# Longer weight runs, quarter-lane casts on two engines, and another order of loads in a batched matrix product

## Chip, cores, metric

One core of one Trainium2 chip (trn2). The metric is the device time of one execution in microseconds (us), median of several executions.

## The reference

```python
b1, b2, m, k, n = 8, 16, 256, 512, 384
x      : (8, 16, 256, 512) float32
weight : (8, 16, 512, 384) float32
return np.matmul(x, weight).astype(np.float32)
```

That is 128 independent products of 256x512 by 512x384. The kernel works on 32 groups of G = 4 products. A group loads 2.10 MB of x and 3.15 MB of weights and stores 1.57 MB.

## The kernel before

Five engines run their own programs and meet at semaphores (counters that one engine raises and another waits for). SyncE (SP) issues all transfers. ScalarE (ACT) casts x to bf16 and copies results out of PSUM, the memory that TensorE writes its results to. VectorE (DVE) casts weights and copies the transposed x out of PSUM. TensorE (PE) transposes and multiplies. GpSimd only makes the identity matrix for the transposes.

```python
def load(e, t, U, s):                       # SP: w, w, x
    n = t * U + s
    for d in range(G // D):                 # two loads of two products each
        slot = (s * (G // D) + d) % WS
        if not isinstance(n, int) or n >= 2:
            e.wait_ge(w_cast, n * (G * S) + ((d + 1) * D * S - 2 * G * S))
        e.dma_start(w_sb[slot][:],          # 128 partitions, 8 rows of w each: 12 KB runs
            w_rows[...].rearrange("(p k) n -> p k n", k=S * KO)).then_inc(w_in[slot], 16)
    ...                                     # then x, 16 KB runs
def prepare(e, t, U, s):                    # DVE
    ...
    for a in range(D):
        for h in range(S):                  # 8 casts per group, each 64 lanes x 1536
            e.tensor_copy(out=w_bf[...][h * HP : (h + 1) * HP],
                          in_=w_sb[slot][a * HP : (a + 1) * HP, h * KO : (h + 1) * KO, :],
                          ).then_inc(w_cast, 1)
    for q in range(T): ...                  # 4 copies x_t <- pt
def on_sync(e):
    ...
    for s in range(U):
        load(e, t, U, LAG + s)              # LAG = 4 groups ahead
        store(e, t, U, s)
def on_scalar(e):
    ...                                     # 4 casts x_bf <- x_sb, then 4 copies out_sb <- po
```

Of the kernel before, what the change touches and what calls it, by code (L numbers as in the profile page):

```python
# [12 lines left out]
def kernel(  # L13
# [6 lines left out]
    nc = tc.nc  # L20
    P = 128

    b1, b2, M, K = x.shape
    _, _, _, N = weight.shape
    B = b1 * b2
    KO = K // P

    x_rows = x.rearrange("b1 b2 m k -> (b1 b2 m) k")
    w_rows = weight.rearrange("b1 b2 k n -> (b1 b2 k) n")
    o_rows = out.rearrange("b1 b2 m n -> (b1 b2 m) n")  # L30

    fp32 = mybir.dt.float32
    bf16 = mybir.dt.bfloat16
# [3 lines left out]



    G = 4  # L40
    C = P // G
    R = G * M // P
    T = R // 2
    D = 2
    S = 2
    HP = P // D
    NG = B // G

    XS, WS, OS = 2, 2 * G // D, 4
    BS, TS, WBS = 1, 2, 2 * G  # L50
    PT, PO = 4, 2

    LAG = 4

    ctx.enter_context(tc.tile_critical(no_gpsimd_drain=True))  # L55

    def sbuf(name, shape, dtype, n):
        return [
            ctx.enter_context(nc.sbuf_tensor(f"{name}{s}", shape, dtype)) for s in range(n)
        ]  # L60
# [6 lines left out]
    def sems(name, n):  # L67
        return [tc.alloc_semaphore(f"{name}{s}") for s in range(n)]
# [2 lines left out]
    identity = sbuf("identity", [P, P], fp32, 1)[0]  # L71
    x_sb = sbuf("x_sb", [P, R, K], fp32, XS)

    x_bf = sbuf("x_bf", [P, R, S, HP, KO], bf16, BS)
    x_t = sbuf("x_t", [P, R, KO // 2, P, 2], bf16, TS)
    w_sb = sbuf("w_sb", [P, S * KO, N], fp32, WS)
    w_bf = sbuf("w_bf", [P, KO, N], bf16, WBS)
    out_sb = sbuf("out_sb", [P, R, N], fp32, OS)
    pt = psum("pt", [P, 2, KO // 2, P], fp32, PT)
# [2 lines left out]



    id_done, x_cast, w_cast, t_made, t_copied, p_made, o_copied = (
        sems(name, 1)[0]
        for name in (
            "id_done", "x_cast", "w_cast", "t_made", "t_copied", "p_made", "o_copied"
        )
    )  # L90
    x_in, w_in, o_out = sems("x_in", XS), sems("w_in", WS), sems("o_out", OS)


    BIAS = 8


    def load(e, t, U, s):
        n = t * U + s
        for d in range(G // D):
            slot = (s * (G // D) + d) % WS  # L100
            if not isinstance(n, int) or n >= 2:
                e.wait_ge(w_cast, n * (G * S) + ((d + 1) * D * S - 2 * G * S))
            e.dma_start(  # L103
                w_sb[slot][:],
                w_rows[bass.ds(n * (G * K) + d * (D * K), D * K)].rearrange(
                    "(p k) n -> p k n", k=S * KO
                ),
            ).then_inc(w_in[slot], 16)
        if not isinstance(n, int) or n >= XS:
            e.wait_ge(x_cast, n * T + (1 - XS) * T)  # L110
        e.dma_start(  # L111
            x_sb[s % XS][:],
            x_rows[bass.ds(n * (G * M), G * M)].rearrange("(p r) k -> p r k", r=R),
        ).then_inc(x_in[s % XS], 16)

    def store(e, t, U, s, pieces=1):
        n = t * U + s
        dram = o_rows[bass.ds(n * (G * M), G * M)].rearrange("(p r) n -> p r n", r=R)
        for q in range(pieces):
            rows = slice(q * R // pieces, (q + 1) * R // pieces)  # L120
            e.wait_ge(o_copied, n * T + ((q + 1) * T // pieces + BIAS))
            e.dma_start(out=dram[:, rows], in_=out_sb[s % OS][:, rows]).then_inc(
                o_out[s % OS], 16
            )

    def cast_x(e, t, U, s, q):
        n = t * U + s
        if q == 0:
            e.wait_ge(x_in[s % XS], (t * (U // XS) + s // XS) * 16 + 16)
        e.wait_ge(t_made, n * T + (q + 1 - T + BIAS))  # L130
        rows = slice(2 * q, 2 * q + 2)
        e.copy(  # L132
            out=x_bf[s % BS][:, rows],
            in_=x_sb[s % XS][:, rows].rearrange("p r (q s c) -> p r s q c", s=S, c=KO),
        ).then_inc(x_cast, 1)

    def prepare(e, t, U, s):
        n = t * U + s
        e.wait_ge(p_made, n * T + (BIAS - T))
        for d in range(G // D):  # L140
            slot = (s * (G // D) + d) % WS
            e.wait_ge(
                w_in[slot], (t * (U * G // D // WS) + s * G // D // WS) * 16 + 16
            )
            for a in range(D):
                for h in range(S):
                    e.tensor_copy(  # L147
                        out=w_bf[(s * G + d * D + a) % WBS][h * HP : (h + 1) * HP],
                        in_=w_sb[slot][a * HP : (a + 1) * HP, h * KO : (h + 1) * KO, :],
                    ).then_inc(w_cast, 1)  # L150
        for q in range(T):
            e.wait_ge(t_made, n * T + (q + 1 + BIAS))
            e.tensor_copy(  # L153
                out=x_t[s % TS][:, 2 * q : 2 * q + 2],
                in_=pt[(s * T + q) % PT][:].bitcast(bf16),
            ).then_inc(t_copied, 1)

    def multiply(e, t, U, s):
        n = t * U + s
        words = x_bf[s % BS][:].rearrange("p r s q c -> p r (s q c)").bitcast(fp32)  # L160
        for q in range(T):
            e.wait_ge(x_cast, n * T + (q + 1))
            e.wait_ge(t_copied, n * T + (q + 1 - PT + BIAS))
            for rr in range(2):
                for h in range(KO // 2):
                    ins = e.transpose(  # L166
                        pt[(s * T + q) % PT][:, rr, h, :],
                        words[:, 2 * q + rr, h :: KO // 2],
                        identity[:],
                    )  # L170
            ins.then_inc(t_made, 1)
        e.wait_ge(w_cast, n * (G * S) + G * S)
        for q in range(T):
            e.wait_ge(t_copied, n * T + (q + 1 + BIAS))
            e.wait_ge(o_copied, n * T + (q + 1 - PO + BIAS))
            for rr in range(2):
                for ko in range(KO):
                    for i in range(G):
                        mine = slice(i * C, (i + 1) * C)
                        ins = e.matmul(  # L180
                            po[(s * T + q) % PO][mine, rr, :N],
                            x_t[s % TS][:, 2 * q + rr, ko // 2, mine, ko % 2],
                            w_bf[(s * G + i) % WBS][:, ko, :],
                            start=(ko == 0),
                            stop=(ko == KO - 1),
                        )
            ins.then_inc(p_made, 1)

    def copy_out(e, t, U, s, q):
        n = t * U + s  # L190
        if q == 0:
            e.wait_ge(o_out[s % OS], (t * (U // OS) + s // OS) * 16 + 16)
        e.wait_ge(p_made, n * T + (q + 1 + BIAS))  # L193
        e.copy(  # L194
            out=out_sb[s % OS][:, 2 * q : 2 * q + 2, :],
            in_=po[(s * T + q) % PO][:, :, :N],
        ).then_inc(o_copied, 1)
# [7 lines left out]
    def on_sync(e):  # L205
        U = OS
        for n in range(LAG):
            load(e, 0, NG, n)
        rounds = (NG - LAG) // U
        with e.Fori(0, rounds) as t:  # L210
            for s in range(U):
                load(e, t, U, LAG + s)
                store(e, t, U, s)
        for n in range(rounds * U, NG):
            if n + LAG < NG:
                load(e, 0, NG, n + LAG)
            store(e, 0, NG, n, T if n == NG - 1 else 1)
        for s in range(OS):
            e.wait_ge(o_out[s], 16 + 16 * (NG // OS + (T - 1 if s == (NG - 1) % OS else 0)))

    def on_vector(e):
        U = 2
        e.sem_inc(t_copied, BIAS)
        with e.Fori(0, NG // U) as t:
            for s in range(U):
                prepare(e, t, U, s)

    def on_tensor(e):
        U = 2
        e.sem_inc(t_made, BIAS)  # L230
        e.sem_inc(p_made, BIAS)
        e.wait_ge(id_done, 2)

        pe = mybir.EngineType.PE
        with nc.Fori(0, NG // U, engines=OrderedEngineSet([pe]), head_slot={pe: 0}) as t:
            for s in range(U):
                multiply(e, t, U, s)

    def on_scalar(e):
        U = OS  # L240
        e.sem_inc(o_copied, BIAS)
        for s in range(OS):
            e.sem_inc(o_out[s], 16)

        with e.Fori(0, NG // U) as t:
            for s in range(U):
                for q in range(T):
                    cast_x(e, t, U, s, q)
                for q in range(T):
                    copy_out(e, t, U, s, q)  # L250

    on_gpsimd(nc.gpsimd)
    on_sync(nc.sync)
    on_vector(nc.vector)
    on_tensor(nc.tensor)
    on_scalar(nc.scalar)


# [28 lines left out]
```

## Time and profile before

| | before |
|---|---|
| time, median of 4 | 518.26 us (517.97 to 518.42) |
| span of the profiled run | 517.2 us (that run took 518.98 us) |
| DMA queue, share of 16 engines | 99.3% |
| DVE, ACT, PE busy | 64%, 46%, 59% |

The lines behind this table stand in the prediction below. The reader should take one thing from them: the 16 DMA engines are busy throughout, and every other engine waits on them.

### The profile page before, as it was taken

The numbers are of one execution on the slowest core, as the hardware profiler recorded it, in microseconds if no ns is written. First come the engines' busy times: TensorE is split into PE (matmuls) and PEld (weight loads), VectorE is DVE, ScalarE is ACT, GpSimd is POOL, SyncE is SP. The second block draws the span as 40 slices with busy tenths as digits, with TensorE's granted clock in tenths as the row PEclk, the third lists the DMA queues.
The fourth block names the chain that finished last, engine by engine and source line by source line (L and its number), as shares of the span: only waits on it lengthen the run. The fifth ranks groups of instructions, "written<-read, shape, count | busy, mean of one in ns | idle before, by whom it ended". The sixth has DMA issues, their size and how long they took to land.

```text
span 517.2 us, 11523 instructions
## 1 busy us (share of the span) xinstructions
PE 306.6 (59%) x4608; PEld 200.6 (39%) x4608; DVE 332.8 (64%) x384; ACT 236.7 (46%) x264; POOL 0.7 (0%) x6
## 2 busy tenths in 40 slices
PE   0478776556665457645577554776446765467752
PEld 0345444334443334433344332444324443244431
DVE  3698875667556676556675566855658656676550
ACT  0465564443644436435355354454444544544441
POOL 0000000000000000000000000000000000000000
PEclk9998877878777887878777778877788877778777
DMA  8999999999999999999999999999999999999996
GB/s 340 430 423 424 424 432 426 429 428 430 432 427 427 427 428 432 429 427 430 426 431 431 426 429 430 427 432 427 427 429 429 427 433 425 430 428 430 429 428 251
DMA packets 18869, 218.18 MB, mean 422 GB/s; under 512 B 2096, under 2 KB 2096, under 8 KB 2608
## 3 DMA queue, kind: packets, MB, share of 16 engines
q1 hardware_dynamic: 18864, 218.11, 99.3%
q8 instruction: 3, 0.05, 0.0%
q14 instruction: 2, 0.02, 0.0%
HBM read 167.77 MB, written 50.33 MB: 422 GB/s over the span
## 4 chain that ended last, share of the span: by engine, by line
DMA 81%; ACT 10%; PE 4%; issue 3%; ACTq 0%; SPq 0%
DMA x_sb<-in_x_dram 81%; ACT x_bf L132 9%; PE po L180 2%; PE pt L166 1%; ACTq L130 0%; ACT out_sb L194 0%; SPq L111 0%; SPq L103 0%; ACT L132 0%; ACTq L193 0%; SPq L282 0%; SPq L55 0%
## 5 line engine op out<-in xcount | busy, mean ns | idle before, releaser
L147 DVE CAST w_bf<-w_sb 64x1536 bf16<-64x1536 f32 x256 | 244.4, 955 | 47.2 <-DMA w_sb<-in_weight_dram 38.5
L166 PE MATMUL pt<-identity,x_bf 128*128 128x128 f32 x512 | 123.7, 425 | 199.3 <-ACT x_bf L132 199.1
L180 PE MATMUL po<-w_bf,x_t 128*32 128x384 bf16 x4096 | 185.1, 342 | 1.0 <-issue 1.0
L166 PEld LDWEIGHTS pt<-identity,x_bf 128*128 128x128 f32 x512 | 91.8, 216 | 232.1 <-issue 218.3
L194 ACT COPY out_sb<-po 128x768 f32<-128x768 f32 x128 | 102.2, 798 | 147.2 <-PE po L180 147.2
L153 DVE COPY x_t<-pt 128x1024 bf16<-128x1024 bf16 x128 | 88.4, 691 | 122.3 <-PE pt L166 121.8
L132 ACT CAST x_bf<-x_sb 128x1024 bf16<-128x1024 f32 x128 | 124.4, 1042 | 80.9 <-DMA x_sb<-in_x_dram 80.8
L180 PEld LDWEIGHTS po<-w_bf,x_t 128*32 128x32 bf16 x4096 | 108.8, 101 | 73.8 <-issue 14.2
L132 ACT ACT_TABLE_LOAD x8 | 10.3, 1283 | 42.9 <-DMA x_sb<-in_x_dram 42.9
masks.py:199 POOL TENSOR_SCALAR_AFFINE_SELECT identity<-identity 128x128 f32<-128x128 f32 x1 | 0.3, 292 | 0.2 <-POOL identity L200 0.2
L200 POOL MEMSET identity<- 128x128 f32 x1 | 0.2, 204 | 0.5 <-SPq L55 0.5
L271 POOL MEMSET const-bfloat16-1.0<- 128x1 bf16 x1 | 0.1, 101 | 0.0
L271 POOL MEMSET const-uint8-127<- 128x1 uint8 x1 | 0.1, 101 | 0.0
L271 POOL MEMSET const-float32-0.0<- 128x1 f32 x1 | 0.1, 98 | 0.2 <-issue 0.2
L271 POOL MEMSET const-float32-1.0<- 128x1 f32 x1 | 0.1, 98 | 0.0
## 6 DMA issues: line engine op xcount, KB each, us to landing
w_sb<-in_weight_dram SPq DMA_DIRECT2D x64, 1536.0 KB, 27.5
x_sb<-in_x_dram SPq DMA_DIRECT2D x32, 2048.0 KB, 27.5
out_dram<-out_sb SPq DMA_DIRECT2D x31, 1536.0 KB, 30.7
out_dram<-out_sb SPq DMA_DIRECT2D x4, 384.0 KB, 5.9
```

The lines of the kernel that those rows point to most:

```text
L132: e.copy(out=x_bf[s % BS][:, rows], in_=x_sb[s % XS][:, rows].rearrange("p r (q s c) -> p r s q c", s=S, c=KO),).then_inc(x_cast, 1)
L147: e.tensor_copy(out=w_bf[(s * G + d * D + a) % WBS][h * HP : (h + 1) * HP], in_=w_sb[slot][a * HP : (a + 1) * HP, h * KO : (h + 1) * KO, : ...
L153: e.tensor_copy(out=x_t[s % TS][:, 2 * q : 2 * q + 2], in_=pt[(s * T + q) % PT][:].bitcast(bf16),).then_inc(t_copied, 1)
L166: ins = e.transpose(pt[(s * T + q) % PT][:, rr, h, :], words[:, 2 * q + rr, h :: KO // 2], identity[:],)
L180: ins = e.matmul(po[(s * T + q) % PO][mine, rr, :N], x_t[s % TS][:, 2 * q + rr, ko // 2, mine, ko % 2], w_bf[(s * G + i) % WBS][:, ko, :], ...
L194: e.copy(out=out_sb[s % OS][:, 2 * q : 2 * q + 2, :], in_=po[(s * T + q) % PO][:, :, :N],).then_inc(o_copied, 1)
L200: e.memset(identity[:], 0.0).then_inc(id_done, 1)
L271: nc = _bacc.Bacc("TRN2", target_bir_lowering=False, num_devices=1)
```

## The change

The intent is fewer and longer packets: one weight load per group with 24 KB runs (16 rows of w per partition) in place of two with 12 KB runs. A product then lies on 32 partitions, so a group needs 16 casts of 32 lanes; 12 go to DVE and 4 to ACT. To make room, the cast of x moves to DVE and the copy of the transposed x to ACT. SP issues x, store, weights. The first four and last two groups keep 12 KB runs and half-lane casts.

```diff
-    def load(e, t, U, s):                  # w (2 x 12 KB runs), then x
+    def load_x(e, t, U, s): ...
+    def is_short(n):
+        return isinstance(n, int) and (n < LAG or n >= NG - 2)
+    def load_w(e, t, U, s):
+        ...
+        d = SL // SH if is_short(n) else 1         # SL, SH = 4, 2
+        k = SL * KO // d                           # 16 rows: 24 KB runs; 8: 12 KB
...
-        e.copy(out=x_bf...)                # ACT
+        e.tensor_copy(out=x_bf...)         # DVE
...
+    def cast_w(e, t, U, s, parts, first=True):     # 32 lanes each
+        copy = e.tensor_copy if e is nc.vector else e.copy
+        for c in parts:
+            i, h = c // SL, c % SL
+            copy(out=w_bf[(s * G + i) % WBS][h * C : (h + 1) * C],
+                 in_=w_sb[s % WS][i * C : (i + 1) * C, h * KO : (h + 1) * KO, :],
+            ).then_inc(w_vcast if c < CV else w_acast, 1)
...
             for s in range(U):
-                load(e, t, U, LAG + s)
+                load_x(e, t, U, LAG + s)
                 store(e, t, U, s)
+                load_w(e, t, U, LAG + s)
```

(Cut: waits, the half-lane form cast_short, the unrolled first and last groups.)

## The prediction

> **What bounds the kernel now.** I first read the page's slices and queue table, because a kernel that loads and stores this much (218 MB for 32 groups) is suspected of being bound by its transfers.
>
> ```profile
> PE 306.6 (59%) x4608; PEld 200.6 (39%) x4608; DVE 332.8 (64%) x384; ACT 236.7 (46%) x264; POOL 0.7 (0%) x6
> ...
> DMA  8999999999999999999999999999999999999996
> ...
> q1 hardware_dynamic: 18864, 218.11, 99.3%
> ```
>
> No engine is busy over 64%, but the DMA row is 9 in every slice but the first and the last, and the queue's packets took 99.3% of what 16 engines have. Next the stretches of the span, to see whether that share is a saturated queue or an average:
>
> ```profile
> 100.00:200.00 100.00, 60.36 (x880) 40.35 (x878) 64.47 (x75) 47.32 (x53) 0.00 (x0) 0.77 1.01 429
> 200.00:300.00 100.00, 64.38 (x982) 41.32 (x984) 66.50 (x78) 45.94 (x52) 0.00 (x0) 0.79 1.01 429
> 300.00:400.00 100.00, 57.86 (x884) 37.99 (x872) 66.52 (x77) 46.06 (x52) 0.00 (x0) 0.80 1.01 429
> ```
>
> The last two columns are DMA share and GB/s: 1.01 and 429 in each, so the queue never runs dry. A group moves 2.097 MB of x, 3.146 MB of weights and 1.573 MB of output, 6.816 MB; at 429 GB/s that is 15.9 us, and the landings of x in the trace are indeed 15.88 us apart. The chain that ended last says the same, and the waits of the issuing queue say why there is always something queued:
>
> ```profile
> DMA 81%; ACT 10%; PE 4%; issue 3%; ACTq 0%; SPq 0%
> ...
> w_sb<-in_weight_dram SPq DMA_DIRECT2D x64, 1536.0 KB, 27.5
> x_sb<-in_x_dram SPq DMA_DIRECT2D x32, 2048.0 KB, 27.5
> ```
>
> A load lands 27.5 us after its issue: 1.7 groups of work stand in the queue. The ACT 10% in the chain is the cast of x that frees x_sb; it runs while the queue is full, so it isn't lost time. At the end the last x lands at 496.6 us and the engines are through at 507.7 us, but stores are still queued until the last packet at 515.4 us. By the trace's landings the 16 DMA engines finish some 3.5 us apart, since they drift (a few were delayed early on by instruction-fetch packets of about 1 us each), and I find no idle gap on the last one. So the time is: 2.0 us before the first packet, one DMA engine's packets back to back (513.4 us), 1.8 us of closing.
>
> **What the Trainium skill says.** "DMA: Bandwidth & Descriptors", section "Where 436 GB/s comes from", gives 16 ports x 32 B x 850 MHz = 435.2 GB/s as ceiling. The 429 GB/s of the trace are 98.6% of it: there is at most 1.4%, some 7 us, to gain from any shape of transfer. The same page, "Why small descriptors are slow", names a fixed overhead of about 3 cycles per packet. The trace agrees in kind: its packet records show 3 KB in 121 ns, 12 KB in 460 ns and 16 KB in 612 ns, nearly proportional to size. A group has 32 data packets and four 9 ns semaphore packets per DMA engine; at 27.2 GB/s their bytes take 15.66 us, measured are 15.88, so (220 - 36) / 32 = 5.8 ns are lost per data packet (an estimate). "VectorE: DVE Perf Modes", "The perf-mode tier table", gives fp32 SBUF copies twice one element per cycle at 0.96 GHz: 1536 elements are 800 ns plus a fixed part, and the trace has 955 ns, so the fixed part is 155 ns here. "ScalarE: Activation LUTs", "What ACT_TABLE_LOAD costs", gives 186 ns + 0.833 ns per element: 1039 ns for 1024; the trace has 1042.
>
> **The change part by part.**
>
> ```profile
> L147 DVE CAST w_bf<-w_sb 64x1536 bf16<-64x1536 f32 x256 | 244.4, 955 | 47.2 <-DMA w_sb<-in_weight_dram 38.5
> ...
> L194 ACT COPY out_sb<-po 128x768 f32<-128x768 f32 x128 | 102.2, 798 | 147.2 <-PE po L180 147.2
> L153 DVE COPY x_t<-pt 128x1024 bf16<-128x1024 bf16 x128 | 88.4, 691 | 122.3 <-PE pt L166 121.8
> L132 ACT CAST x_bf<-x_sb 128x1024 bf16<-128x1024 f32 x128 | 124.4, 1042 | 80.9 <-DMA x_sb<-in_x_dram 80.8
> ```
>
> (1) Transfers. In 26 of 32 groups two weight loads of 12 KB runs become one of 24 KB runs: 26 x 256 packets become 26 x 128, that is 3328 fewer, 208 per DMA engine, and 26 semaphore packets fewer per engine. Bytes stay. Gain on the path: 208 x 5.8 ns = 1.2 us, and 26 x 9 ns = 0.2 us; in all 1.4 us.
>
> (2) Casts of weights. 32 lanes take as long as 64 (each lane has 1536 elements), so a group of 24 KB runs needs 16 casts where 8 did. 12 go to DVE, at the 7.86 / 8 = 0.98 us spacing that the trace shows for such casts: 11.8 us. 4 go to ACT at 1042 + 512 x 0.833 = 1468 ns: 5.9 us.
>
> (3) The cast of x moves from ACT to DVE: 4 per group. At the rate of the weight cast, 1024 / 1.92 + 155 = 688 ns, 2.8 us. The copy of x_t moves from DVE to ACT: 4 of 798 + 256 x 0.833 = 1011 ns, 4.0 us. copy_out stays, 4 x 0.80 = 3.2 us.
>
> (4) Sums per group: DVE 11.8 + 2.8 = 14.6 us, before 4 x 0.69 + 7.86 = 10.6. ACT 5.9 + 4.0 + 3.2 = 13.1 us. Both fit in the 15.9 us that the transfers take, DVE by only 1.3 us. Over the whole kernel I expect DVE at 26 x 12 x 0.955 + 48 x 0.955 + 128 x 0.69 = 432 us (84%) and ACT at 104 x 1.468 + 128 x (1.011 + 0.798) = 384 us (74%).
>
> (5) Does the queue stay full? Let w of group n land at time 0. Its casts end at 11.8, and only then w of n+2 may be issued. Behind w of n stand x of n+1 (4.9 us), a store (3.7), w of n+1 (7.3), x of n+2 (4.9) and a store (3.7): the queue would ask for w of n+2 at 24.4. Spare: 24.4 - 11.8 - about 2 for issue = 10.6 us. The coarser slot is paid from a queue that is deep enough.
>
> (6) Ends. At the start, x first lets casts begin with x, while five more loads are queued: no gap. At the end w of group 31 lands last, in two halves. From then: 4 casts of the second half 3.9 us, multiplication to the first quarter 1.5, copy 0.8; the last of four pieces is issued about 10.2 us after landing. In the queue are stores 28, 29, 30 (11 us) and three pieces (2.8): the slowest DMA engine comes to the last piece at 13.8. Still no gap, 3 us spare.
>
> (7) The unrolled first and last groups make the programs of DVE and ACT longer; every further instruction fetch delays one DMA engine by about 1.3 us, which counts if it is the last one. I put 0 to 1.5 us on it, 0.6 in the middle.
>
> Sum: 518.1 - 1.4 + 0.6 = 517.3 us. The change buys back a descriptor cost that is almost nothing, with engine time that is free as long as it fits.
>
> **The rivals.** (a) *DVE becomes the bound.* If the strided fp32 read of the x cast (runs of 4 elements) ran at one element per cycle, it would take 1067 + 155 = 1222 ns, and DVE 11.8 + 4.9 = 16.7 us per group, over 15.9. 26 groups x 0.8 = 21 us, of which the 10.6 us of queue depth hide half: about 527 us. For it speaks the thin margin; against it that ACT reads the same pattern at full rate, and that both outermost counts are even, so the pattern should split over two ports. I give it 8%. (b) *Larger runs are faster than the per-packet sum says*, because of the memory's side: at most the way to 435 GB/s, -7 us, 511 us. Against it: 12 KB and 16 KB packets show no gain per byte beyond the few ns. 5%. (c) *The tail or the coupling of ACT and DVE leaves gaps*: ACT's quarter casts stand between copies out, so a late weight holds the copies, PE and the next transposes. 2 to 5 us, 520 to 523. 12%; the 10.6 us of spare speak against it in the middle, less so at the end.
>
> **Range and chances.** The middle case spans 516 to 518.5 with runs that differ by 0.45 us; (b) stretches it down to 515, (c) up to 521. Faster by 2% would be under 507.8, below what 435 GB/s allows together with both ends (501.2 + 3.8 = 505.0 and drift of some 3): 2%. Slower by 2% needs rival (a): 5%.
>
> **What would show it.** Right: data and semaphore packets 15120 instead of 18864; share and GB/s in the middle unchanged or 430; 24 KB packets at about 915 ns; x cast on DVE near 690 ns and quarter cast near 955 ns; DVE about 84%, ACT about 74%, chain still mostly DMA. Wrong: x cast near 1.2 us with DVE over 95% (a); GB/s at 433 or more (b); slices of DMA under 9 in the last two or in the middle (c).

## More of the kernel before

What the page averages away is that the 16 DMA engines don't keep step. Each transfer ends with one semaphore increment from every DMA engine, and the trace holds the time of each. I call **lag** the time between the first and the last of a transfer's 16 increments. In the kernel before it is 2.1 us on the first load and 3.4 us near the end.

## The result

The changed kernel took 518.76 us (median of 4, 518.70 to 519.21) against 518.26. A ratio here is the mean time of one kernel's runs over that of the other's of the same rounds, so not quite the ratio of the medians quoted: 1.0012, 95% interval 0.9995 to 1.0029. That is no difference. The two profiled runs differ the other way, 516.9 against 517.2 us of span, since the profile of before fell on a run of 518.98 us; nothing under half a microsecond should be read from those two spans.

The page of the changed kernel, busy time, DMA share and queue:

```profile
PE 304.8 (59%) x4608; PEld 207.1 (40%) x4608; DVE 422.4 (82%) x488; ACT 370.7 (72%) x361; POOL 0.7 (0%) x6
...
DMA  8999999999999999999999999999999999999995
...
q1 hardware_dynamic: 15120, 218.11, 98.9%
```

The packets are 3744 fewer, as counted beforehand, and DVE and ACT do 90 and 134 us more. The DMA row is the same. The costliest groups of the changed kernel (count, busy us and mean ns, then idle time before them):

```profile
L160 DVE CAST w_bf<-w_sb 32x1536 bf16<-32x1536 f32 x312 | 296.7, 951 | 57.7 <-DMA w_sb<-in_weight_dram 48.8
L228 ACT COPY out_sb<-po 128x768 f32<-128x768 f32 x128 | 102.0, 797 | 121.3 <-PE po L214 120.7
L160 ACT CAST w_bf<-w_sb 32x1536 bf16<-32x1536 f32 x104 | 152.6, 1468 | 8.2 <-DMA w_sb<-in_weight_dram 6.3
L186 ACT COPY x_t<-pt 128x1024 bf16<-128x1024 bf16 x128 | 120.3, 1025 | 0.6
L147 DVE CAST x_bf<-x_sb 128x1024 bf16<-128x1024 f32 x128 | 80.0, 689 | 13.7 <-DMA x_sb<-in_x_dram 12.8
```

32 lanes cost 951 ns where 64 cost 955: twice the casts for the same data. The strided cast of x runs on DVE in 689 ns, so rival (a) of the prediction is out. Stretches of the changed kernel (the last two columns are DMA share and GB/s; the DVE column is the third after the length):

```profile
100.00:200.00 100.00, 61.18 (x953) 41.30 (x948) 87.01 (x101) 78.12 (x75) 0.00 (x0) 0.80 1.00 430
200.00:300.00 100.00, 61.40 (x907) 41.51 (x896) 88.17 (x102) 80.62 (x77) 0.00 (x0) 0.80 1.01 432
300.00:400.00 100.00, 59.20 (x872) 39.74 (x876) 87.72 (x102) 80.03 (x78) 0.00 (x0) 0.78 1.01 430
...
505.00:510.00 5.00, 5.00 (x80) 2.96 (x76) 0.00 (x0) 1.33 (x2) 0.00 (x0) 0.61 0.48 199
510.00:515.00 5.00, 2.02 (x52) 1.16 (x43) 0.00 (x0) 1.88 (x3) 0.00 (x0) 1.00 0.62 243
```

The middle moves 430 to 432 GB/s where it was 429. The end is new. The same two stretches of the kernel before:

```profile
505.00:510.00 5.00, 1.87 (x48) 1.01 (x40) 0.00 (x0) 1.72 (x3) 0.00 (x0) 1.00 0.98 409
510.00:515.00 5.00, 0.00 (x0) 0.00 (x0) 0.00 (x0) 0.00 (x0) 0.00 (x0) 0.64 0.44 177
```

Before, the last 10 us were only stores draining, with PE through by 507 us. Now PE still multiplies until 512 us and the DMA engines are half idle. The chain that ended last, in order of time, shows why PE is late in the changed kernel (start, length, what):

```profile
479.61 16.63 DMA w_sb<-in_weight_dram
...
504.46 7.59 PE po L214 x97
512.05 0.02 issue
512.07 0.80 ACT out_sb L228
```

Weights are loaded last now, so cast, multiplication and copy of the last group follow that landing.

The landings tell where the microseconds of the longer runs went. Store 30, the last full store, was complete on the fastest DMA engine at 506.13 us, before at 507.68: **1.55 us sooner, about what was forecast**. On the slowest it was complete at 511.44 us, before at 512.05: only 0.61 us sooner. The lag at that store had grown from 4.37 to 5.30 us. So the question for the experiments is what sets the time, and what sets the lag.

### The profile page after: what moved, and what is told of

Same layout as the page of the kernel before. It is cut to its first block, busy times and chain, and to the rows that moved or that the text cites. A ratio compares the mean times of both kernels' runs of the same rounds, so it can differ in the third digit from the quotient of the medians.

```text
span 516.9 us, 11527 instructions
## 1 busy us (share of the span) xinstructions
PE 304.8 (59%) x4608; PEld 207.1 (40%) x4608; DVE 422.4 (82%) x488; ACT 370.7 (72%) x361; POOL 0.7 (0%) x6
## 4 chain that ended last, share of the span: by engine, by line
DMA 60%; DVE 26%; issue 10%; PE 2%; DVEq 1%; SPq 0%; ACT 0%
DMA w_sb<-in_weight_dram 60%; DVE w_bf L160 20%; DVE w_bf L176 6%; PE po L214 2%; DVEq L272 0%; SPq L123 0%; DVEq L144 0%; ACT out_sb L228 0%; SPq L106 0%; DVEq L156 0%; DVEq L170 0%; SPq L352 0%; SPq L58 0%
## 5 line engine op out<-in xcount | busy, mean ns | idle before, releaser
L214 PE MATMUL po<-w_bf,x_t 128*32 128x384 bf16 x4096 | 235.7, 405 | 196.4 <-DVE w_bf L160 146.0
L160 DVE CAST w_bf<-w_sb 32x1536 bf16<-32x1536 f32 x312 | 296.7, 951 | 57.7 <-DMA w_sb<-in_weight_dram 48.8
L214 PEld LDWEIGHTS po<-w_bf,x_t 128*32 128x32 bf16 x4096 | 141.9, 117 | 283.9 <-ACT x_t L186 181.7
L160 ACT CAST w_bf<-w_sb 32x1536 bf16<-32x1536 f32 x104 | 152.6, 1468 | 8.2 <-DMA w_sb<-in_weight_dram 6.3
L186 ACT COPY x_t<-pt 128x1024 bf16<-128x1024 bf16 x128 | 120.3, 1025 | 0.6
L147 DVE CAST x_bf<-x_sb 128x1024 bf16<-128x1024 f32 x128 | 80.0, 689 | 13.7 <-DMA x_sb<-in_x_dram 12.8
L199 PE MATMUL pt<-identity,x_bf 128*128 128x128 f32 x512 | 71.2, 293 | 10.9 <-DVE x_bf L147 10.9
L199 PEld LDWEIGHTS pt<-identity,x_bf 128*128 128x128 f32 x512 | 65.1, 209 | 20.7 <-issue 20.7
L176 DVE CAST w_bf<-w_sb 64x1536 bf16<-64x1536 f32 x48 | 45.8, 955 | 10.4 <-DMA w_sb<-in_weight_dram 7.8
## 6 DMA issues: line engine op xcount, KB each, us to landing
w_sb<-in_weight_dram SPq DMA_DIRECT2D x26, 3072.0 KB, 19.8
```

The lines of the kernel that those rows point to most:

```text
L147: e.tensor_copy(out=x_bf[s % BS][:, rows].rearrange("p r (s q c) -> p r s q c", s=S, c=KO), in_=x_sb[s % XS][:, rows].rearrange("p r (q s ...
L160: copy(out=w_bf[(s * G + i) % WBS][h * C : (h + 1) * C], in_=w_sb[s % WS][i * C : (i + 1) * C, h * KO : (h + 1) * KO, :],).then_inc(w_vcas ...
L176: e.tensor_copy(out=w_bf[(n * G + d * SH + a) % WBS][h * p : (h + 1) * p], in_=w_sb[n % WS][a * p : (a + 1) * p, r : r + KO, :],).then_inc ...
L186: e.copy(out=x_t[s % TS][:, 2 * q : 2 * q + 2], in_=pt[(s * T + q) % PT][:].bitcast(bf16),).then_inc(t_copied, 1)
L199: ins = e.transpose(pt[(s * T + q) % PT][:, rr, h, :], words[:, 2 * q + rr, h :: KO // 2], identity[:],)
L214: ins = e.matmul(po[(s * T + q) % PO][mine, rr, :N], x_t[s % TS][:, 2 * q + rr, ko // 2, mine, ko % 2], w_bf[(s * G + i) % WBS][:, ko, :], ...
```

## The experiments

**Theory A**: the transfers bind. The span is the packet stream of the slowest DMA engine, a packet costs its bytes and a few ns, and the added engine work is hidden while it fits under 15.9 us per group. Rivals: packets' shape is free and waits bind (B); the order and the exchange of engines cost something that the long runs give back (C); the tail binds (D).

### e1: many more packets

```diff
-            e.dma_start(w_sb[slot][:], w_rows[...]).then_inc(w_in[slot], 16)
+            for j in range(4):              # 3 KB runs; the wait on w_in is for 64 instead of 16
+                e.dma_start(w_sb[slot][:, 2*j : 2*j+2, :], w_rows[...][:, 2*j : 2*j+2, :]
+                ).then_inc(w_in[slot], 16)
```

> The kernel before, with each 12 KB weight run cut into four 3 KB runs (four transfers each). Theory A (the span is one DMA engine's packets back to back, and a packet costs its bytes plus some 5 ns): 1536 more data packets per engine, 13.5 ns more per 12 KB by the packet records (4 x 117.5 against 456.5) x 512 = 6.9 us, and 192 more semaphore packets x 9 ns = 1.7 us: 518.3 + 8.6 = about 527 us. Rival B (the shape of runs is free, and the span is held by the chain x landing, cast, slot free): unchanged, 518 us.

Measured: 532.43 us (before 518.15), ratio 1.0271. The shape of runs is not free (rival B falls), and it cost 14.3 us where 8.6 were expected: 14.3 us over 1728 added packets per DMA engine (192 of them semaphore packets) is **8.3 ns per packet**. Most of the excess lies in the sizes put in: the expectation had 117.5 and 456.5 ns for packets of 3 and 12 KB, where the records of the kernel before show medians of 121 and 460. With these, 512 x (4 x 121 - 460) = 12.3 us and 1.7 us of semaphore packets make 14.0. SyncE had 192 more transfers to issue, but the DMA engines did not run dry waiting for it: their share stays at 1.02 while the rate falls to 418 GB/s from 429.

```profile
200.00:300.00 100.00, 58.85 (x870) 38.69 (x871) 62.42 (x73) 46.93 (x53) 0.00 (x0) 0.76 1.02 418
```

Scaled to the change, 234 packets fewer are worth 1.9 us at this price. That is an estimate, but the size agrees with the 1.55 us seen on the fastest DMA engine.

### e2: the change without its long runs

```diff
-        return isinstance(n, int) and (n < LAG or n >= NG - 2)
+        return True                          # cast_short in every group, indices made general
```

> The changed kernel with 12 KB runs and half-lane casts in every group: order and exchange of engines stay, the long runs go. Theory A: the 1.4 us of 208 packets come back, 518.8 + 1.4 = about 520 us. Rival B (order and exchange of engines are what costs the half microsecond, long runs give nothing): as the changed kernel, 518.8 us. Rival C (quarter-lane casts eat a gain of the long runs): the engines get spare time but the gain goes too, 518.3 as the kernel before.

Measured: 524.85 us, ratio 1.0128 (1.0112 to 1.0143). **Every theory missed**: not 520, and neither 518.8 nor 518.3. Read simply, the long runs are worth 6 us and the rest of the change costs 6.6. But the middle of this run moves 428 to 429 GB/s as before; what is new lies at its end (stretches):

```profile
400.00:480.00 80.00, 46.87 (x716) 31.84 (x712) 49.95 (x60) 34.34 (x40) 0.00 (x0) 0.80 1.01 430
...
505.00:510.00 5.00, 0.03 (x1) 0.00 (x0) 4.84 (x6) 2.45 (x3) 0.00 (x0) 0.73 0.71 297
510.00:515.00 5.00, 4.20 (x64) 2.58 (x68) 0.56 (x1) 0.80 (x1) 0.00 (x0) 0.59 0.06 25
515.00:520.00 5.00, 2.80 (x72) 1.72 (x60) 0.00 (x0) 2.39 (x3) 0.00 (x0) 1.00 0.72 283
```

At 510 us nearly nothing is left to transfer while DVE and PE still prepare the last group. Its weights landed on the fastest DMA engine at 496.7 us and on the slowest at 506.3: the lag is 9.6 us. It grew by 0.32 us in each group. Going through the landings by transfer, the slowest DMA engine takes as long as the others for loads of x (4.88 us against 4.89) and of weights (3.68 and 3.68), but 3.94 us for its share of a store where the median takes 3.7. Only stores, and only that one DMA engine.

This made **theory H**. For each store I counted the TensorE instructions (all its records in the trace, nearly all of them matmuls and weight loads) that began while the slowest DMA engine did its share. Over six kernels (before, changed, e2 to e5), from where this DMA engine is the slowest, its share takes 3723 ns + 2.0 ns per TensorE instruction, with a correlation of 0.945. Much of that rests on e2: without it, a recount over the stores from 250 us on gives 0.77 to 0.90, by how many of the last stores are taken in. In e2 there are 99 to 143 such instructions because multiplication begins right after 8 casts and falls into the store; in the changed kernel 0 to 23 until the last groups.

### e9: the same with more work, later

```diff
+            if d == 0 and not (isinstance(n, int) and n >= NG - 2):
+                for j in range(4):           # useless casts to a scratch tile
+                    e.tensor_copy(out=spare[s % 2][j * C : (j + 1) * C],
+                                  in_=w_sb[s % WS][:C, :KO, :])
```

> All groups with 12 KB runs and half-lane casts, as the run of that name before, with four useless casts per group on DVE (into a scratch tile) ahead of the weight casts, so that multiplication starts 3.9 us later. Theory H (one DMA engine loses time in its share of each store in proportion to the TensorE instructions that run meanwhile: over six kernels the traces give 3723 ns + 2.0 ns per instruction, correlation 0.945; in the all-short kernel multiplication falls into that store): TensorE instructions in the store fall from 105 to about 30, 0.15 us per group come back, 4 to 4.5 us in all: about 520.5 us with MORE work. Rival L (the 24 KB runs themselves are worth the 6 us): 525 us or more.

Measured: 519.33 us, ratio 1.0019 (1.0006 to 1.0033). Against e2's ratio of 1.0128, **some 5.6 us were gained by adding 120 useless casts**. The page of e9:

```profile
PE 304.8 (59%) x4608; PEld 206.8 (40%) x4608; DVE 438.0 (85%) x504; ACT 221.2 (43%) x257; POOL 0.7 (0%) x6
...
q1 hardware_dynamic: 18864, 218.11, 99.4%
```

The packets are those of e2, 18864. TensorE instructions in the slowest engine's store fell from 108 to 14 (means of the last nine stores of the middle), the store's share from 3936 to 3701 ns, the lag near the end from 9.3 to 2.9 us. So the long runs are not worth 6 us (rival L falls): with the lag gone, kernels with and without them differ by well under a microsecond (ratios to before 1.0012 and 1.0019). Part of what the long runs save is hidden in that comparison, since e9 has the smaller lag at store 30, 4.1 us against 5.3.

### e3 and e4: the tail

```diff
-        return isinstance(n, int) and (n < LAG or n >= NG - 2)      # e3: long runs to the end
+        return isinstance(n, int) and n < LAG
```

> The changed kernel with 24 KB runs and quarter-lane casts in the last two groups too (the first four stay short). Theory A: the tail has no spare left: after the last landing, 16 quarter casts on two engines take about 11.8 us where 4.3 were, so the end moves by 7.5 us less about 1 of queue: 525 us. Rival (the queue of stores hides it): 518.5 us.

Measured: 525.23 us, ratio 1.0129. As forecast: the half-lane casts of the last two groups are worth 6.5 us, because the last weights then come in two halves and only the second half's four casts follow the last landing.

```diff
             if n + LAG < NG:
                 load_x(e, 0, NG, n + LAG)
+            if n + LAG == NG - 1:
+                load_w(e, 0, NG, n + LAG)
             store(e, 0, NG, n, T if n == NG - 1 else 1)
-            if n + LAG < NG:
+            if n + LAG < NG - 1:
                 load_w(e, 0, NG, n + LAG)
```

> The changed kernel with the last weight load issued ahead of store 27 instead of behind it. The last cast, multiplication and copy then start 3.7 us sooner, the transfers are the same. Theory A (the slowest DMA engine runs without a gap to the end): unchanged, 518.8 us, though the fast engines idle less in the last 10 us. Rival D (the tail is held by cast, multiplication and copy of group 31): up to 3 us less, 516 us.

Measured: 518.60 us, ratio 1.0008 (0.9994 to 1.0021): unchanged. Its last stretches:

```profile
505.00:510.00 5.00, 0.92 (x24) 0.41 (x16) 0.00 (x0) 1.27 (x2) 0.00 (x0) 0.96 0.95 390
510.00:515.00 5.00, 0.00 (x0) 0.00 (x0) 0.00 (x0) 0.00 (x0) 0.00 (x0) 0.50 0.14 57
```

Against the 0.48 and 199 GB/s of the changed kernel, the gap from 505 to 510 us is filled, PE is through well before 510 us, and the time stays. The gap was idle time of the 15 faster DMA engines. In the changed kernel the slowest one finished store 30 at 511.44 us and the four quarter stores at 512.44, 513.44, 514.39 and 515.30, one after the other. So the tail of engine work alone does not set the time (rival D). But it stands right behind the lag: in the changed kernel the last copy out ended at 512.87 us, and the 15 faster DMA engines, which had waited for it, landed the last piece at 515.03 to 515.21 us, 0.1 us ahead of the slowest. e3 shows what a longer tail costs.

### e5 to e8: does the added cast work fit?

```diff
         copy = e.tensor_copy if e is nc.vector else e.copy
+        if e is nc.vector:
+            for j in range(1):               # e5; range(3) in e6
+                copy(out=spare[s % 2][j * C : (j + 1) * C], in_=w_sb[s % WS][:C, :KO, :])
```

> The changed kernel with one useless quarter-lane cast more on DVE in each of the 26 groups of long runs (into a scratch tile). DVE then has about 11.8 + 2.8 + 1.0 = 15.6 us per group against 15.9 of the transfers. Theory A: it fits, 519 us. Rival (the added casts are on the path): 26 x 0.98 = 25 us, 544 us.

> The same with three useless casts per group: DVE 17.5 us per group, 1.65 over the transfers. Theory A: 26 x 1.65 = 43 us, less some 10.6 of queue depth: about 551 us, DVE over 95% busy. Rival (on the path from the first): 26 x 2.9 = 76 us, 595 us. If the margin was larger than predicted: near 519.

Measured: e5 519.86 us (ratio 1.0026), e6 546.29 us (1.0533). One cast more per group, 25 us of work in all, costs about 1 us (0.7 by the ratios 1.0026 and 1.0012, whose intervals overlap); three cost 27.5. A stretch of e5, then of e6:

```profile
200.00:300.00 100.00, 59.79 (x916) 40.80 (x907) 92.95 (x107) 80.10 (x77) 0.00 (x0) 0.80 1.01 431
```

```profile
200.00:300.00 100.00, 57.18 (x864) 38.86 (x864) 97.60 (x112) 73.27 (x71) 0.00 (x0) 0.80 1.00 398
```

DVE at 93% still leaves the transfers at 431 GB/s; at 97.6% they fall to 398 GB/s, 17.1 us per group. The added work of the change is hidden, and the limit is near.

```diff
+            if pieces == 1:                  # e7 on the kernel before, e8 on the changed one
+                rows = slice(0, R // 2)      # wrong on purpose: half of each store is left out
```

> The kernel before with every full store cut to its first half (wrong result on purpose): 0.786 MB less per group, 31 groups. Theory A: 31 x 0.786 MB / 429 GB/s = 57 us less, 461 us. Rival (held by engines or waits): 518 us or a part of it.

> The changed kernel with every full store cut to its first half (wrong result on purpose). Its transfers need 14.05 us per group, its DVE 14.6: theory A with the working of step 4 makes DVE the bound, 26 x 0.55 = 14 us, less some of the queue depth, over the kernel before with half stores: 466 to 475 us. If DVE's real need is lower (the profile has 689 ns and 951 ns for the two casts, and overlaps), 461 us as the other.

Measured: e7 464.43 us, e8 469.67 us (468.35 to 471.83). Their outputs are wrong, which doesn't matter for the times. With 24.4 MB less the kernel before gets 54 us faster: 57 would be the bytes at 429 GB/s. At its end the quarter stores land with a lag of only 0.17 us, so there the DMA engines do wait for the last group, behind whose work fewer stores stand. Theory A holds at nearly full size. e8 is within its range, but not by the mechanism that I had named:

```profile
100.00:200.00 100.00, 66.00 (x996) 43.84 (x991) 97.34 (x114) 87.57 (x85) 0.00 (x0) 0.83 1.01 431
200.00:300.00 100.00, 67.36 (x1029) 44.36 (x1025) 97.38 (x113) 88.40 (x85) 0.00 (x0) 0.83 1.01 430
```

DVE is at 97% but the transfers still run at 430 GB/s, so DVE is not yet the bound; it needs at most 14.0 us per group, not 14.6. What differs is the lag, 6.6 us near the end against 2.8 in e7. In e8 the slowest engine's half stores took about 2.1 us in the middle of the run, with some 80 instructions of all engines beginning in each, against 1.89 us and about 15 in e7.

### e10 and e11: leaving the slowest DMA engine out, failed

```diff
+            cuts = ((0, 120), (120, 128)) if isinstance(n, int) and n == 28 else ((0, 128),)
+            for a, b in cuts:                # n == 27 in e11, on the changed kernel
+                e.dma_start(out=dram[a:b, rows], in_=out_sb[s % OS][a:b, rows]
+                ).then_inc(o_out[s % OS], 16)
```

> The kernel before with store 28 cut in partitions 0 to 119 and 120 to 127, which goes by 15 and by 8 DMA engines. Theory A (the end is the end of the slowest DMA engine's queue): if that engine is the one left out by the first part, it does 3.65 us less while eight others do 0.46 more; it was 2 us behind the next, so the end comes some 1.5 to 2 us sooner: 516.5 us. If the slowest is another engine, 518.2 to 518.8.

> The changed kernel with the same cut of store 27, which stands ahead of the last weight load. If the left-out engine is the slowest, the last weights land up to 2.5 us sooner and the slowest queue ends so much sooner: 516.3 us, better than both kernels. If not: 518.8 to 519.3.

Measured: e10 522.53 us (ratio 1.0079), e11 519.50 us (1.0019). In e11 one DMA engine landed the next load 3 us ahead of all others, so one was left out, but it was not the slowest, which still came last. And the store over 120 partitions was slow for the others: in e11 the other fifteen landed the next store on average some 1.2 us later than the spacing of the changed kernel gives (the part over 8 partitions explains at most 0.25 of it), and the longest 12 KB packet took 1868 ns (2232 in e10) where 460 is usual. No gain, and no version that beats both kernels.

### e12: more TensorE instructions, inconclusive

```diff
-            for rr in range(2):
+            for rr in (0, 1, 0, 1):          # every transpose twice
```

> The kernel before with every transpose made twice on TensorE (the same words to the same place, result unchanged); transfers and casts stay. Its transposes fall into the slow DMA engine's share of the store. Theory H (2.0 ns per TensorE instruction that runs meanwhile): about 28 instructions more per store, so that store takes some 3810 ns on that engine where 3755 were, its lag before the last stores is about 4.8 us where 3.4 were, and the time 519.7 us. Rival (the lag has to do with the phase of the casts, not with the number of TensorE instructions): store times as before, lag 3.4, 518.3 us.

Measured: 519.41 us, ratio 1.0015 (1.0001 to 1.0028), lag 4.0 us before the last stores. The premise failed: the doubled transposes spread over a longer time, so that the store saw 29 TensorE instructions instead of 26, not 28 more (means of the last nine). The store took 3761 ns against 3748. That is within theory H but no test of it, and most of the larger lag stood already at 100 us.

## Why the prediction was right, and where it wasn't

**The bound** was right: e7 takes bytes away and the time follows; e4 to e6 move engine work about and it doesn't, until DVE is full.

**Step 1** (fewer packets, -1.4 us) was right in size where it can be seen, on the fastest DMA engine (1.55 us). The price of 5.8 ns per packet was low: e1 gives 8.3, and the changed kernel's records 8 (two packets of 460 ns against one of 912).

**Steps 2 to 4** (costs of casts and sums) held: 951 ns, 1468 ns, 689 ns measured for about 955, 1468 and 688; 1025 for 1011. DVE 422 us and ACT 371 us against 432 and 384. DVE's need was put too high by more than half a microsecond per group (the four casts of x take 2.50 us back to back, not 2.8).

**Step 5** (the queue stays full) held: 430 to 432 GB/s. The DMA issues of the changed kernel show how much nearer it runs (us to landing in the last column):

```profile
w_sb<-in_weight_dram SPq DMA_DIRECT2D x26, 3072.0 KB, 19.8
x_sb<-in_x_dram SPq DMA_DIRECT2D x32, 2048.0 KB, 22.2
```

The depth is 19.8 us where it was 27.5, for the weights have to wait for all 16 casts of their slot.

**Step 6** (ends) had the right verdict for the wrong reason. I gave multiplication 1.5 us for its first quarter and 3 us of spare. PE's granted clock was 0.61 there and the whole multiplication took 7.6 us. The last copy out ended 13.0 us after the last weights had landed (512.87 against 499.89), not 10.2. The slowest DMA engine had no gap only because it was so late: with a smaller lag it would have waited for that copy as the others did, and the end would have come 0.1 us sooner at most. No run takes both the lag and the tail away.

**Step 7** (instruction fetches) was right in kind: one further 8 KB instruction packet shows at 422.5 us, absent before, and the lag rises from 3.3 to 4.0 us with the load of x that it falls into. It hit just the slowest DMA engine. It cost 0.7 us (309 ns, and 410 ns on the data packet behind it), not the 1.3 of the working; the 0.6 in the sum was close.

**The sum** was out by little here. In the one profile of each kernel the last increment came at 515.30 us against 515.77, 0.5 us sooner where the sum had 0.8: 1.55 us on the fastest DMA engine, less a lag 0.9 us larger at store 30 (0.7 of it from the fetch), less 0.1 us over the quarter stores. The medians put the changed kernel 0.5 us behind instead; the profiled run of before was a slow one for its kernel, and the rest of that difference is not explained.

**What the working lacked** is the lag as something that can change. I treated it as a constant, "they drift", from the kernel before. By e2 and e9 it depends on when the casts and the multiplication fall against the store. In steady state the queue's cycle of transfers is the same (weights, x, store); what moved is where the engines' work falls in it. In e2, the same change without long runs, the lag near the end is 6 us larger. The range held because the lag stayed small here, which I had not worked out: that was luck.

Open: why one DMA engine's stores suffer while TensorE runs. e9 shows that shifting the casts and multiplication against the store removes the lag, and the fit says by how much per TensorE instruction; since other engines' instructions shift too, it isn't shown that TensorE itself is the cause, nor whether the recording of instructions in these runs has a part in it.

## What to carry to other kernels

When the DMA row is at 9 throughout, first ask how far the rate is from its ceiling: here 1.4% by the prediction's working, so no change of run length could be expected to be worth more, whatever it costs in instructions. A transfer is complete when the slowest of 16 DMA engines is, so look at the spread of a transfer's landings over time, not only at the mean share; a spread that grows can be paid in full at the end, as in e2, unless the end waits for engine work anyway. And work that is hidden now is not free: one more cast of 1 us per group passed here, three cost 27 us.

## What the Trainium skill lacked or had wrong

- "DMA: Bandwidth & Descriptors", "Why small descriptors are slow", has about 3 cycles per packet, beside 32 bytes of descriptor metadata per operation. e1 paid 8.3 ns per added packet, with its longer records and semaphore packets in it, more than twice the 3 cycles if they are those of the 850 MHz fabric named on the same page (3.5 ns, an estimate).
- "SBUF — State Buffer", "SBUF: two separate sides", says that a compute op cannot slow a DMA. In these runs one DMA engine's share of a 1.5 MB store took 3.70 us with 14 TensorE instructions beginning meanwhile and 3.94 us with 108, and over 31 groups this came to some 6 us of the span. Whether it is SBUF where they meet is not shown, nor whether it is TensorE's work or the recording of it, so this doubts the sentence and does not refute it.
- "DMA: Bandwidth & Descriptors", "Latency and other measured facts", knows slower DMA engines, with a best guess tied to descriptors that GpSimd writes. Here nearly all packets are on the queue that the profile calls hardware_dynamic, and one DMA engine is slower all the same, in stores alone. Its number is not in the trace.
- No page that I read has the cost of an instruction packet to the transfers: a 16 KB one took about 1.1 us, the data packet behind it some 0.47 us longer than usual, and one DMA engine stayed behind by that. One of 8 KB took 309 ns and cost the slowest DMA engine 0.7 us.
- No page that I read has the price of a store over 120 partitions: in e11 the DMA engines that took part landed the next store on average some 1.2 us late after one such store of 1.4 MB.
